# One wide Strassen unit for the values of four retention heads, placed early, in place of two narrow ones

## The chip, the core and the metric

One core of a Trainium2 chip runs the whole program. Its engines work side by side, each through its own list of instructions in order: TensorE (PE) multiplies matrices, VectorE (DVE) and ScalarE (ACT) do elementwise work, GpSimd (POOL) and SyncE (SP) mostly issue transfers. Results of TensorE land in PSUM, which the program uses as 8 banks of 128 partitions by 512 fp32. The metric is the device time of one execution in microseconds, the median of several.

## The reference

A decoder block on 512 tokens of width 1024, cut to what matters here:

```python
h = rmsnorm(x, norm1_w)
proj = h @ w_in                       # 1024 x 6656
rq, rk, rv, rg, mq, mk, mv, ga, gb = split(proj)
rq, rk = rotary(rq), rotary(rk) * RET_DK**-0.5
ret = silu(rg) * retention(rq, rk, rv)        # 4 heads, rv: 256 columns a head, group-normalised
a = ret @ w_ret_out
b = moba_attention(rmsnorm(mq), rmsnorm(mk), mv) @ w_moba_out     # 8 heads of 64
x = x + (sigmoid(ga) * a + sigmoid(gb) * b) @ w_o
h2 = rmsnorm(x, norm2_w)
x = x + (silu(h2 @ w_ffn_gate) * (h2 @ w_ffn_up)) @ w_ffn_down
```

The change concerns `rv`, the 1024 columns of values of the four retention heads.

## The kernel before

Every fp32 operand is kept as a high and a low part, and each product is three matmuls (`mm3`: high x high, high x low, low x high). Most projections run as Strassen units in Winograd's form: seven products B11, T1, T2, B21, B22, T3, T4 of quarter matrices in place of eight. The strings of lines 80 to 84 give their order within a unit; what stands behind the "/" is deferred, and the next unit runs it at its "*1". In the order NORMAL the copy of B11's result seeds the Z bank (`p1`), so that B21 adds onto it there.

A product adds up in a PSUM bank called X, Y, Z (or W), by the table in `wino_unit`. A narrow unit (`cols`, half 256) takes 512 columns of `w_in`; its matmuls are 256 columns wide, and a product needs one bank. A wide unit (half 512) takes 1024 columns; its matmuls are 512 wide, and a product needs two banks. In either there are 168 matmuls (7 products, 8 steps of `mm3`), 12 at a narrow tick and 6 at a wide one: 14 ticks in a narrow unit, 28 in a wide one. Before the change one unit of this part is wide: `mv_ev`, which makes attention's values and half of the retention gates. The bank `zbank` is held for good; of `zbanks` a second one is kept for the first wide unit (`bank`). All other banks come in turn from one pool of eight, for products (`main_ps`, named `pm` in the rows) and for everything else (`side_ps`, named `ps`).

At each tick three things happen: weight pieces move on (`advance`: a ScalarE cast gives the high part `wh`, VectorE's subtraction from it the low part `wl`, and weight sums `raw` + `raw` make T2 and T4), work that was put off comes due (`later`), and one background step is taken from the list `bg` (`run_bg`). The background is attention first: scores of a pair of heads (`att_products`), maxima and exponentials (`att_scores`), transpositions (`att_transpose`, copies `pt` at lines 1130 and 1135), values (`att_values`). Behind it follow the retention scores and values of two heads each (`ret_scores`, `ret_values`), which `rv_out` appends when its unit has given its last result, and `ret_finish` when all four parts in `due` are done.

The order of the units is the list `ORDER` (line 45): a unit of queries and keys, `("rv", 0)`, a gate unit, queries and keys again, `("rv", 1)`, then the others. `weight_plan` puts down the same order for the transfers. A narrow rv unit hands each of its four quarters, two token tiles of one head, to `split`, which makes its high and low parts.

Of the kernel before, what the change touches and what calls it, by code (L numbers as in the profile page):

```python
# [13 lines left out]
ALU = mybir.AluOpType  # L14
# [25 lines left out]
STARTERS = 2  # L40
EXTRA = 1
WIDE = 4
OEXTRA = 5
FEXTRA = -2
ORDER = (("rk", 0), ("rv", 0), ("gb", 0), ("rk", 1), ("rv", 1), ("rg", 1), ("gb", 1), ("b", 0), ("b", 1), ("ga", 0), ("a", 0), ("ga", 1), ("a", 1))
RLAG = (1, 2, 3)
SLAG = (1, 1, 1)
ROT = 1
# [32 lines left out]
ENDING = "B11 T1 *1 T2 B21 B22 T3 T4w"  # L81
PLAIN = "B11 B21 B12 B22"
DOWN = "B11 B21 T1 T2 B22 T3 / T4"
ALONE = "B11 B21 T1 T2 B22 T3 T4z"


def weight_plan():

    units = []

    def feat(blocks):
        assert len(blocks) % 16 == 0  # L100
        for i in range(0, len(blocks), 16):
            units.append(("F", blocks[i:i + 16]))

    def group(name, col, kts):
        return [(name, k * P, col) for k in range(kts)]

    def wino(name1, col1, name2, col2, order=NORMAL):
        quarters = ((name1, col1, 0), (name2, col2, 0), (name2, col2, 4), (name1, col1, 4))
        units.append(("W", [(n, (k0 + k) * P, c + i * P) for n, c, k0 in quarters for i in (0, 1) for k in range(4)],
                      order))  # L110

    halves = (range(4), range(4, 8))

    def cols(col):
        units.append(("X", ("w_in", halves, (col, col + 256), 256), NORMAL))

    units += [("M", (C_MQ, 0)), ("M", (C_MQ, 4)), ("M", (C_MK, 0)), ("M", (C_MK, 4))]
    units.append(("X", ("w_in", halves, (C_MV, C_RG), 512), NORMAL))
    for name, i in ORDER:
        if name == "rg":  # L120
            cols(C_RG + 512 * i)
        elif name == "rv":
            cols(C_RV + 512 * i)
        elif name == "rk":
            wino("w_in", C_RQ + 256 * i, "w_in", C_RK + 256 * i)
        elif name == "a":
            feat(sum([group("w_ret_out", (4 * i + ct) * P, KT) for ct in range(4)], []))
        elif name == "b":
            feat(sum([group("w_moba_out", (4 * i + ct) * P, 4) for ct in range(4)], []))
        else:  # L130
            c = {"ga": C_GA, "gb": C_GB}[name] + 512 * i
            wino("w_in", c + 256, "w_in", c)
    units.append(("X", ("w_o", halves, (0, 512), 512), ALONE))
    for c in range(len(CHUNKS)):
        fs = chunk_tiles(c)
        for f in fs[::2]:
            order = ENDING if f == fs[-2] else NORMAL
            if f < 4:
                order = (PLAIN, DOWN)[f // 2]
            wino("w_ffn_gate", f * P, "w_ffn_up", f * P, order)  # L140
        units.append(("X", ("w_ffn_down", (fs[::2], fs[1::2]), (0, 512), 512), ALONE if c == len(CHUNKS) - 1 else DOWN))
    return units
# [27 lines left out]
def hybrid_block(ctx: ExitStack, tc: tile.TileContext, wall, xin, xtok, n2, cin, out):  # L170
# [642 lines left out]
    def wino_unit(w, ev, hooks={}):  # L813

        u = cur[0]
        cur[0] += 1
        order = plan[u][2].split()
        wide = plan[u][0] == "X" and plan[u][1][3] == 512
        banks = {}

        def bank(b):
            if b not in banks:
                z = zbank if b == "Z" else main_ps()
                banks[b] = [z, zbanks.pop() if b == "Z" and len(zbanks) > 1 else main_ps()] if wide else z
            return banks[b]

        def third(*x):
            ev.c22(*x)
            if "T4w" in order:
                ev.u3(*x)  # L830

        def first(*x):
            ev.p1(*([*x, bank("Z")] if seed else x))

        whole = "T4w" in order or "T4z" in order
        seed = order[1] != "B21"
        table = {"B11": ("X", "A11", True, False, first), "T1": ("Y", "S1", True, False, ev.p5),
                 "T2": ("X", "S2", False, False, ev.u2), "B21": ("Z", "A12", not seed, True, ev.c11),
                 "B22": ("Y", "S4", False, True, ev.c12), "T3": ("X", "S3", False, whole, third),
                 "T4": ("X", "A22", False, True, ev.c21),  # L840
                 "T4w": ("W", "A22", True, True, getattr(ev, "c21w", None)),
                 "T4z": ("Z", "A22", False, True, ev.c21)}

        def run(q):
            b, m, start, stop, out = table[q]
            wino_prod(w, u, bank(b), m, q.rstrip("wz"), start, stop, out,
                      (lambda i: ev.u3(bank("X"), i, bank("Z"))) if q == "T3" and "T4z" in order else None,
                      q == "T4z")

        rest = False  # L850
        for q in order:
            if q == "/":
                rest = True
            elif q[0] == "*":
                for _ in range(int(q[1:])):
                    wino_finish()
            elif rest:
                wpend.append(lambda q=q: run(q))
            else:
                run(q)  # L860
                if q in hooks:
                    hooks[q]()
# [53 lines left out]
    class WideQuarters:  # L916


        def __init__(self, out):
            self.out = out  # L920
            self.tiles = big(nm("qa")), big(nm("qb"))
            self.a, self.b = ((t[:, :512], t[:, 512:]) for t in self.tiles)

        def p1(self, x, i, z):
            A.copy(z[i], x[i])

        def p5(self, y, i):
            A.activation(self.a[i], y[i], AF.Copy, scale=-1.0)
# [2 lines left out]
            A.activation(self.b[i], x[i], AF.Copy, scale=-1.0)  # L931

        def c11(self, z, i):
            self.out(0, 0, i, z[i])

        def c12(self, y, i):
            V.tensor_tensor(self.b[i], self.b[i], y[i], ALU.subtract)
# [268 lines left out]
    def rot_out(h0):  # L1206
        def f(r, c, x):

            a, b = halves(nm("rot"))
            hf = RDK // 2  # L1210
            cos, sin = (y[:, r * 256:(r + 1) * 256].unsqueeze(1).to_broadcast([P, 2, 256]) for y in (cosT, sinT))
            part = {}

            def turn():
                A.copy(b[:hf], x[hf:])
                A.copy(b[hf:], x[:hf])

            def same():
                V.tensor_tensor(two(a), two(x), cos, ALU.mult)

            def high():
                if (c, h0) not in rT:
                    H, L = big(f"rH{c}_{h0}", F32R), big(f"rL{c}_{h0}", F32R)
                    rT[c, h0] = H, L
                    for i in (0, 1):
                        s = slice(i * 512, (i + 1) * 512)
                        (rqT, rkT)[c][h0 + i] = Two(H[:, s], L[:, s])
                part["H"], part["L"] = (two(y)[:, :, r * 256:(r + 1) * 256] for y in rT[c, h0])
                A.copy(part["H"], two(a))

            d = lane_start(LANE)
            if c == 0 or d == 0:
                turn()
            else:
                later(d, turn)
            later(1 if c == 0 else d + 1, same)
            later(d + 1, lambda: V.tensor_tensor(two(b), two(b), sin, ALU.mult))
            later(d + 2, lambda: V.tensor_tensor(a, a, b, ALU.add))
            later(d + 3, high)
            later(d + 4, lambda: V.tensor_tensor(part["L"], two(a), part["H"].bitcast(F32), ALU.subtract))  # L1240
        return f

    rqT, rkT = {}, {}
# [1 line left out]

    rv = {}

    def rv_out(h0):
        def f(pair, i, x):
            rv[h0 + i, pair] = split(f"rv{h0 + i}_{pair}", x, None, 0 if i == 0 else SLAG[1])  # L1250
            if (pair, i) == (1, 0):
                a, b = ([lambda h=h, j=j: ret_scores(h, j) for j in range(NT)] for h in (h0, h0 + 1))
                v, w = ([lambda h=h, p=p: ret_values(h, p) for p in range(2)] for h in (h0, h0 + 1))
                fs = gates(h0 // 2)
                bg.extend(a + fs[:3] + v + b + [fs[3], None, None] + w + [None])
                ret_done("rv")
        return f


    sk = small("sk", RH * NT, 1)  # L1260
# [44 lines left out]
    def ret_values(h, pair):  # L1305
        ps = side_ps()
        for i in (2 * pair, 2 * pair + 1):
            c = (i % 2) * 256
            for j in range(i + 1):
                key, off = sc_off[j]  # L1310
                o = off + (i - j) * P
                mm3(ps[:, c:c + 256], tuple(x[:, o:o + P] for x in sc[h, key]),
                    rv[h, j // 2][:, (j % 2) * 256:(j % 2) * 256 + 256], j == 0, j == i)
        def stats():
            for i in (0, 1):
                bs = tp.tile([P, 6], F32, name=nm("bs"), tag="bs", bufs=4)
# [55 lines left out]

    def rk_unit(n):
        wino_unit(hW, Quarters(rot_out(2 * n)))

    def rv_unit(n):
        wino_unit(hW, Quarters(rv_out(2 * n)))


    sga, sgb, mixT = {}, {}, {}  # L1380
# [74 lines left out]
    def branch(cts, n, mov, evac):  # L1455
# [2 lines left out]
        feat_blocks(blocks[:n] + [wino_finish] + blocks[n:])  # L1458

    make = {  # L1460
        "rg": rg_unit, "rk": rk_unit, "rv": rv_unit,
        "ga": lambda n: gate_unit(sga, 4 * n),
        "gb": lambda n: gate_unit(sgb, 4 * n),
        "a": lambda n: branch(range(4 * n, 4 * n + 4), KT, retT, a_evac),
# [4 lines left out]
    wino_unit(hW, mv_ev)  # L1469
    more_raws(-WIDE)  # L1470
    for name, n in ORDER:
        make[name](n)
    assert not bg


# [362 lines left out]
```

## Time and profile before

| | |
|---|---|
| time, median of 3 runs | 779.18 us (779.07 to 779.64) |
| the profiled execution | 779.37 us, its span 777.6 us |
| granted TensorE clock, mean | 0.999 |
| TensorE, VectorE, ScalarE, GpSimd busy | 99%, 81%, 58%, 9% |
| chain that ended last: TensorE, VectorE, ScalarE | 91%, 4%, 3% |
| moved by transfers | 134.85 MB, 173 GB/s on average |

The span is that of the instructions on the slowest (here the only) core; the execution has 1.77 us around it. Matmuls overlap one another, so the duration of one row is longer than the spacing from one to the next; the spacing is what a matmul costs in a full stream. A row of the timeline can stand for several like instructions (x2, x4), and rows of two kinds overlap where they alternate. In the names `wh` and `wl` are the parts of a weight piece, `hS` and `hA` those of activation sums and quarters, `mk` and `mq` attention's keys and queries, `p` softmax rows, `mx` and `nb` row maxima and what is made of them, `rot` and `rH` rotated queries and keys, `moT` attention's output.

### The profile page before, as it was taken

How to read it: one execution, taken by the hardware profiler on the slowest of the kernel's cores; microseconds unless marked ns; L12 is line 12 of the kernel's file. 1: busy time of each engine (PE TensorE's matmuls, PEld its weight loads, DVE VectorE, ACT ScalarE, POOL GpSimd, SP SyncE). 2: the span in 40 equal slices, each digit the busy share in tenths (PEclk: the TensorE clock that was granted, in tenths of full speed). 3: DMA queues.
4: the chain of work that ended last, by engine and by line, in shares of the span. 5: the costliest groups of instructions: out<-in, count | busy, mean ns of one | idle time of the engine just before them, and what ended most of it. 6: DMA issues, size and time to landing. Idle time of an engine off the chain costs nothing.

```text
span 777.6 us, 13317 instructions
## 1 busy us (share of the span) xinstructions
PE 770.1 (99%) x5226; PEld 702.2 (90%) x5226; DVE 630.9 (81%) x959; ACT 454.7 (58%) x744; POOL 68.7 (9%) x83
## 2 busy tenths in 40 slices
PE   8999999999999999999999999999999999999997
PEld 6888888889999998989988899989999899988996
DVE  6988688987797687758589998899787977789786
ACT  7656587877675485634355775655554455654551
POOL 0001000000101000000001000111001110110000
PEclk9999999999999999999999999999999999999999
DMA  9947542536778475553899714789556993779502
GB/s 324 356 122 186 136 83 56 145 101 163 190 164 203 110 220 117 166 134 119 258 329 248 183 34 116 185 205 304 150 145 156 268 265 99 173 201 294 119 2 109
DMA packets 40671, 134.85 MB, mean 173 GB/s; under 512 B 4512, under 2 KB 5024, under 8 KB 40608
## 3 DMA queue, kind: packets, MB, share of 16 engines
q1 hardware_dynamic: 28512, 93.75, 34.4%
q0 software_dynamic: 11376, 39.06, 28.6%
q10 hardware_dynamic: 720, 1.18, 0.5%
q8 instruction: 41, 0.67, 0.3%
q14 instruction: 22, 0.18, 0.1%
HBM read 131.88 MB, written 2.10 MB: 172 GB/s over the span
## 4 chain that ended last, share of the span: by engine, by line
PE 91%; DVE 4%; ACT 3%; issue 1%; DMA 1%; ACTq 0%
PE pm L222 84%; PE ps L222 8%; DVE h L222 1%; DMA raw<-wall 1%; DVE ws L222 1%; DVE wl L222 1%; ACT wh L418 1%; ACT f L1577 0%; DVE mx L222 0%; ACT p L1098 0%; DVE rot L222 0%; ACT h L1565 0%; DVE gsl L222 0%; ACT L1684 0%; ACT L1098 0%
## 5 line engine op out<-in xcount | busy, mean ns | idle before, releaser
L222 DVE TENSOR_TENSOR wl<-raw,wh 128x1024 fp32r<-128x1024 f32 x209 | 252.5, 1220 | 46.3 <-ACT wh L418 39.4
L418 ACT CAST wh<-raw 128x1024 fp32r<-128x1024 f32 (+1 forms) x230 | 225.6, 1008 | 59.9 <-DVE raw L222 32.4
L222 PE MATMUL pm<-h,wh 128*128 128x256 f32 x1248 | 225.2, 283 | 0.2 <-ACT fa L1650 0.2
L222 PEld LDWEIGHTS pm<-h,wh 128*128 128x128 f32 x1248 | 195.1, 192 | 0.9 <-ACT fa L1650 0.4
L222 PE MATMUL pm<-h,wl 128*128 128x256 f32 x624 | 176.6, 283 | 0.0
L222 PEld LDWEIGHTS pm<-h,wl 128*128 128x128 f32 x624 | 119.7, 192 | 0.0
L345 POOL DMA_DIRECT2D raw<-wall x60 | 53.9, 898 | 453.2 <-DMA raw<-wall 202.9
L222 PE MATMUL pm<-hS,wh 128*128 128x256 f32 x384 | 71.6, 286 | 0.0
L222 PE MATMUL pm<-wh,hA 128*128 128x256 f32 (+1 forms) x256 | 66.8, 337 | 0.0
L222 PEld LDWEIGHTS pm<-hS,wh 128*128 128x128 f32 x384 | 59.9, 191 | 0.3 <-issue 0.2
L222 PE MATMUL pm<-wh,hS 128*128 128x256 f32 (+1 forms) x256 | 57.2, 311 | 0.0
L222 PE MATMUL pm<-hS,wl 128*128 128x256 f32 x192 | 54.3, 283 | 0.0
L222 PE MATMUL pm<-hA,wh 128*128 128x256 f32 x288 | 53.6, 285 | 0.0
L222 DVE TENSOR_TENSOR raw<-raw,raw 128x1024 f32<-128x1024 f32 (+1 forms) x41 | 48.2, 1181 | 0.4
L222 PEld LDWEIGHTS pm<-wh,hA 128*128 128x128 f32 x256 | 44.4, 190 | 4.1
L222 PEld LDWEIGHTS pm<-hA,wh 128*128 128x128 f32 x288 | 45.2, 191 | 0.9 <-issue 0.3
L222 PEld LDWEIGHTS pm<-wh,hS 128*128 128x128 f32 x256 | 42.8, 190 | 2.8 <-issue 0.2
L222 PE MATMUL pm<-wl,hA 128*128 128x256 f32 (+1 forms) x128 | 42.2, 330 | 0.0
L222 PE MATMUL pm<-hA,wl 128*128 128x256 f32 x144 | 40.7, 283 | 0.0
L222 PE MATMUL pm<-wh,gsh 128*128 128x512 f32 x112 | 39.8, 390 | 0.0
L222 PE MATMUL pm<-wl,hS 128*128 128x256 f32 (+1 forms) x128 | 39.6, 309 | 0.0
L222 PE MATMUL pm<-ret,wh 128*128 128x512 f32 x128 | 39.5, 390 | 0.0
(255 smaller groups left out, 1379.6 us busy)
## 6 DMA issues: line engine op xcount, KB each, us to landing
raw<-wall SPq DMA_DIRECT2D x155, 512.0 KB, 5.4
raw<-wall POOLq DMA_DIRECT2D x70, 512.0 KB, 7.2
raw<-wall SPq DMA_DIRECT2D x19, 256.0 KB, 4.0
raw<-wall POOLq DMA_DIRECT2D x9, 256.0 KB, 7.4
xr<-xtok SPq DMA_DIRECT2D x4, 512.0 KB, 7.2
x<-xin SPq DMA_DIRECT2D x7, 256.0 KB, 5.3
out<-xr SPq DMA_DIRECT2D x7, 256.0 KB, 2.1
raw<-wall ACTq DMA_DIRECT2D x4, 256.0 KB, 6.3
```

What stands on the lines that cost most here:

```text
L222: return f(out, *args, **kw)
L345: nc.gpsimd.dma_start(t[:, s], wall[c, :, s], accum_op=ALU.add)
L418: A.copy(h, src)
```

## The change

One unit `rvv` stands in the place of `("rv", 0)` and makes all 1024 columns of `rv`; `("rv", 1)` goes. The unit is wide, with an order of its own, EARLIER, whose B21 is not added onto a seed: `p1` copies B11's two banks into an SBUF tile `qc` (ScalarE), and `c11` adds the Z banks to it (VectorE). During the unit two more weight buffers are in use (`WIDE2`). Its results are split by pair of heads and token tile, heads 2 and 3 forty ticks later (`VLAG`). The background steps of heads 0 and 1 are appended at the unit's end, those of heads 2 and 3 from the last rotation of the second queries-and-keys unit (`ret_heads`).

```diff
-ORDER = (("rk", 0), ("rv", 0), ("gb", 0), ("rk", 1), ("rv", 1), ("rg", 1), ("gb", 1), ...
+ORDER = (("rk", 0), ("rvv", 0), ("gb", 0), ("rk", 1), ("rg", 1), ("gb", 1), ...
+EARLIER = "B11 *1 B21 T1 T2 B22 T3 / T4"
...
+        elif name == "rvv":
+            units.append(("X", ("w_in", halves, (C_RV, C_RV + 512), 512), EARLIER))
...
-        seed = order[1] != "B21"
+        seed = [q for q in order if q[0] not in "*/"][1] != "B21"
...
-        def p1(self, x, i, z):
-            A.copy(z[i], x[i])
+        def p1(self, x, i, z=None):
+            if z:
+                A.copy(z[i], x[i])
+                return
+            if i == 0:
+                self.first[0], self.first[1] = halves(nm("qc"))
+            A.copy(self.first[i], x[i])
...
         def c11(self, z, i):
-            self.out(0, 0, i, z[i])
+            if not self.first:
+                self.out(0, 0, i, z[i])
+                return
+            f = self.first.pop(i)
+            V.tensor_tensor(f, f, z[i], ALU.add)
+            later(1, lambda: self.out(0, 0, i, f))
...
+            if (r, c, h0) == (1, 0, 2):
+                later(d + 5, lambda: ret_heads(2))
...
+    def rv_unit():
+
+        def out(r, c, i, x):
+            t = 2 * r + i
+            later(VLAG if c else 0, lambda: keep(c, t, x))
+            if (r, c, i) == (1, 0, 1):
                 ret_done("rv")
-        return f
+                ret_heads(0)
+
+        def keep(c, t, x):
+            y = split(f"rv{c}_{t}", x, None, SLAG[1])
+            for h in (0, 1):
+                rv[2 * c + h, t] = y, h * 256
+
+        wino_unit(hW, WideQuarters(out))
...
+        if name == "rvv":
+            more_raws(WIDE2)
         make[name](n)
+        if name == "rvv":
+            more_raws(-WIDE2)
```

Three places of the order of instructions show what moved. The first is TensorE's list at the transposition of one head's `p` in the last group of attention, with the unit's products around it; before the change:

```order
L222 MATMUL pm_198_1507<-wh_208_1624,hS41_498 128x256
L222 MATMUL pm_198_1507<-wl_215_1660,hS41_498 128x256
L222 MATMUL pm_198_1507<-wh_208_1624,hS41_498 128x256 x2
L222 MATMUL pm_198_1507<-wl_215_1660,hS41_498 128x256
L222 MATMUL pm_198_1507<-wh_208_1624,hS41_498 128x256
L222 MATMUL ps_236_1853<-cst_79,p_222_1716 128x128 x4
L222 MATMUL pm_188_1420<-wh_219_1698,hS30_526 128x256
```

and after it:

```order
L227 MATMUL pm_236_1759<-wl_221_1639,hS10_415 128x512
L227 MATMUL pm_236_1759<-wh_213_1608,hS10_415 128x512
L227 MATMUL ps_240_1798<-cst_79,p_227_1687 128x128 x4
L227 MATMUL pm_235_1758<-wh_224_1669,hS11_419 128x512
L227 MATMUL pm_235_1758<-wl_228_1697,hS11_419 128x512
L227 MATMUL pm_235_1758<-wh_224_1669,hS11_419 128x512 x2
L227 MATMUL pm_235_1758<-wl_228_1697,hS11_419 128x512
L227 MATMUL pm_235_1758<-wh_224_1669,hS11_419 128x512
L227 MATMUL ps_242_1820<-cst_79,p_230_1711 128x128 x4
L227 MATMUL ps_243_1827<-mk3_832,mq3_562 128x384
L227 MATMUL ps_244_1828<-mk3_832,mq3_562 128x384
```

The transpositions stand beside matmuls of 512 columns now, six at a tick; the first bank they take (`ps_240`) is the one that held `pm_219`, the second Z bank.

The second place is VectorE's list from the row maxima of the group before (`mx` of `ps_221` and of `ps_226`); before the change:

```order
L222 TENSOR_REDUCE mx_1743<-ps_221_1701 128x1
L222 SCALAR_TENSOR_TENSOR nb_1744<-mx_1743,qs_236 128x1
L222 TENSOR_TENSOR rot_214_1657<-rot_214_1657,cs_121 128x512
L222 RECIPROCAL rl_1713<-l_1712 128x1
L222 TENSOR_SCALAR p_222_1716<-p_222_1716,rl_1713 128x512
L222 TENSOR_REDUCE mx_1792<-ps_229_1774 128x1
L222 TENSOR_REDUCE mx_1792<-ps_230_1775 128x1
L222 SCALAR_TENSOR_TENSOR nb_1793<-mx_1792,qs_236 128x2
L222 TENSOR_TENSOR rot_214_1657<-rot_214_1657 128x512
L222 RECIPROCAL rl_1746<-l_1745 128x1
L222 TENSOR_SCALAR p_226_1749<-p_226_1749,rl_1746 128x512
L222 TENSOR_TENSOR wl_232_1819<-raw_179_1360,wh_227_1766 128x1024
```

and after it:

```order
L227 TENSOR_TENSOR rot_220_1636<-rot_220_1636,cs_121 128x512
L227 RECIPROCAL rl_1684<-l_1683 128x1
L227 TENSOR_SCALAR p_227_1687<-p_227_1687,rl_1684 128x512
L227 TENSOR_TENSOR qc_204_1535<-qc_204_1535,pm_17_233 128x512
L227 TENSOR_TENSOR raw_162_1227<-raw_162_1227,raw_180_1362 128x1024
L227 TENSOR_REDUCE mx_1748<-ps_232_1730 128x1
L227 TENSOR_REDUCE mx_1748<-ps_233_1731 128x1
L227 SCALAR_TENSOR_TENSOR nb_1749<-mx_1748,qs_236 128x2
L227 TENSOR_TENSOR rot_220_1636<-rot_220_1636 128x512
L227 RECIPROCAL rl_1708<-l_1707 128x1
L227 TENSOR_SCALAR p_230_1711<-p_230_1711,rl_1708 128x512
L227 TENSOR_TENSOR qc_204_1535<-qc_204_1535,pm_219_1626 128x512
```

Two additions into `qc` and a weight sum `raw` stand in the list; the second addition reads `pm_219`.

The third place is ScalarE's list up to the copies `pt` out of the bank of those transpositions, `ps_236` before the change:

```order
L1098 ACTIVATE p_234_1831,l_1826<-ps_229_1774,nb_1825,qs_236 128x256
L1098 ACTIVATE p_234_1831,l_1826<-ps_230_1775,nb_1825,qs_236 128x256
L1229 CAST rH0_0_1392<-rot_214_1657 128x2x256
L418 CAST wh_235_1851<-raw_203_1582 128x1024
L1130 COPY pt_210_1629<-ps_236_1853 128x2x128
L1135 COPY pt_212_1631<-ps_236_1853 128x256
```

and `ps_240` after it:

```order
L1113 ACTIVATE p_238_1779,l_1774<-ps_232_1730,nb_1773,qs_236 128x256
L1113 ACTIVATE p_238_1779,l_1774<-ps_233_1731,nb_1773,qs_236 128x256
L494 CAST rv0_0_1782<-qc_204_1535 128x512
L1244 CAST rH0_0_1394<-rot_220_1636 128x2x256
L1145 COPY pt_215_1613<-ps_240_1798 128x2x128
L1150 COPY pt_217_1615<-ps_240_1798 128x256
```

A cast of values has come in, and the weight cast stands elsewhere.

## Rows read from the trace of the kernel before

**Rows 1.** The page: busy time of the engines, and the granted clock in 40 slices.

```profile
PE 770.1 (99%) x5226; PEld 702.2 (90%) x5226; DVE 630.9 (81%) x959; ACT 454.7 (58%) x744; POOL 68.7 (9%) x83
PEclk9999999999999999999999999999999999999999
```

**Rows 2.** Waits of TensorE: engine, tile, releaser; us in total, times, longest us.

```profile
PE ps L542 <- DVE warm L222: 1.2, 1, 1.2
...
PE ps L222 <- ACT p L1098: 0.4, 1, 0.4
PE ps L222 <- ACT pt L1135: 0.3, 1, 0.3
...
PE pm L222 <- DVE ml L222: 0.2, 1, 0.2
```

**Rows 3.** TensorE's timeline, two waits: start us, us, instruction, [idle before <- releaser].

```profile
98.09 0.79 PE L222 MATMUL ps<-mk,mq 64*128 64x384 f32 x5 [0.41 <-ACT p L1098]
...
139.44 0.66 PE L222 MATMUL ps<-cst,p 128*128 128x128 f32 x4 [0.29 <-ACT pt L1135]
```

**Rows 4.** TensorE's timeline, matmuls of 256 columns.

```profile
216.08 0.40 PE L222 MATMUL pm<-hS,wh 128*128 128x256 f32 x2
...
216.44 0.40 PE L222 MATMUL pm<-hS,wh 128*128 128x256 f32 x2
```

**Rows 5.** TensorE's timeline, matmuls of 512 columns (the unit `mv_ev`).

```profile
81.05 0.62 PE L222 MATMUL pm<-wh,hS 128*128 128x512 f32 x2
...
81.73 0.62 PE L222 MATMUL pm<-wh,hS 128*128 128x512 f32 x2
```

**Rows 6.** TensorE's timeline: a group's last scores, and the transposition after them.

```profile
144.03 0.96 PE L222 MATMUL ps<-mk,mq 64*128 64x512 f32 x6
...
152.78 0.60 PE L222 MATMUL ps<-cst,p 128*128 128x128 f32 x4
```

**Rows 7.** VectorE's timeline from 145.1 to 154.1 us.

```profile
145.19 0.69 DVE L222 TENSOR_REDUCE mx<-ps 128x1 f32<-128x512 f32 x1 [1.23 <-PE ps L222]
...
146.60 0.68 DVE L222 TENSOR_TENSOR rL<-rot,rH 128x512 fp32r<-128x512 f32 x1
147.19 1.22 DVE L222 TENSOR_TENSOR wl<-raw,wh 128x1024 fp32r<-128x1024 f32 x1
148.33 0.68 DVE L222 TENSOR_REDUCE mx<-ps 128x1 f32<-128x512 f32 x1
...
152.11 1.22 DVE L222 TENSOR_TENSOR wl<-raw,wh 128x1024 fp32r<-128x1024 f32 x1
153.25 0.75 DVE L222 TENSOR_REDUCE mx<-ps 128x1 f32<-128x256 f32 x2
154.03 0.16 DVE L222 SCALAR_TENSOR_TENSOR nb<-mx,qs 128x2 f32<-128x2 f32 x1
```

**Rows 8.** ScalarE's timeline from 154.2 to 157.3 us.

```profile
154.23 0.56 ACT L1098 ACTIVATE p<-ps,nb,qs 128x256 f32<-128x256 f32 x1 [1.37 <-DVE nb L222]
...
155.33 0.61 ACT L1229 CAST rH<-rot 128x512 fp32r<-128x512 f32 x1
155.84 1.05 ACT L418 CAST wh<-raw 128x1024 fp32r<-128x1024 f32 x1
156.78 0.37 ACT L1130 COPY pt<-ps 128x256 f32<-128x256 f32 x1
157.05 0.38 ACT L1135 COPY pt<-ps 128x256 f32<-128x256 f32 x1
```

**Rows 9.** ScalarE's timeline from 127.7 to 129.3 us.

```profile
127.79 1.05 ACT L418 CAST wh<-raw 128x1024 fp32r<-128x1024 f32 x1
128.75 0.36 ACT L1130 COPY pt<-ps 128x256 f32<-128x256 f32 x1
129.01 0.27 ACT L1135 COPY pt<-ps 128x128 f32<-128x128 f32 x1
```

More of the change, by code (lines that the diff above doesn't have):

```diff
@@ L42 @@
 WIDE = 4
+WIDE2 = 2
+VLAG = 40
 OEXTRA = 5
 FEXTRA = -2
-ORDER = (("rk", 0), ("rv", 0), ("gb", 0), ("rk", 1), ("rv", 1), ("rg", 1), ("gb", 1), ("b", 0), ("b", 1), ("ga", 0), ("a", 0), ("ga", 1), ("a", 1))
+ORDER = (("rk", 0), ("rvv", 0), ("gb", 0), ("rk", 1), ("rg", 1), ("gb", 1), ("b", 0), ("b", 1), ("ga", 0), ("a", 0), ("ga", 1), ("a", 1))
 RLAG = (1, 2, 3)
@@ L919, in __init__ @@
         def __init__(self, out):
-            self.out = out
+            self.out, self.first = out, {}
             self.tiles = big(nm("qa")), big(nm("qb"))
             self.a, self.b = ((t[:, :512], t[:, 512:]) for t in self.tiles)
-        def p1(self, x, i, z):
-            A.copy(z[i], x[i])
+        def p1(self, x, i, z=None):
[5 more added lines that the diff above has]
+            A.copy(self.first[i], x[i])
         def p5(self, y, i):
@@ L1246, in hybrid_block, with ret_heads @@
     rv = {}
[L1248 to L1255, printed above, removed]
-                ret_done("rv")
-        return f
+    def rv_unit():
[3 more added lines that the diff above has]
+            if (r, c, i) == (1, 0, 1):
+                ret_done("rv")
+                ret_heads(0)
[4 more added lines that the diff above has]
+        wino_unit(hW, WideQuarters(out))
+    def ret_heads(h0):
+        a, b = ([lambda h=h, j=j: ret_scores(h, j) for j in range(NT)] for h in (h0, h0 + 1))
+        v, w = ([lambda h=h, p=p: ret_values(h, p) for p in range(2)] for h in (h0, h0 + 1))
+        fs = gates(h0 // 2)
+        if h0:
+            bg.extend(a + fs[:2] + v + b + fs[:2] + w)
+            ret_done("rv")
+        else:
+            bg.extend(a + fs[:3] + v + b + [fs[3], None, None] + w + [None])
     sk = small("sk", RH * NT, 1)
@@ L1312, in ret_values @@
                 mm3(ps[:, c:c + 256], tuple(x[:, o:o + P] for x in sc[h, key]),
-                    rv[h, j // 2][:, (j % 2) * 256:(j % 2) * 256 + 256], j == 0, j == i)
+                    rv[h, j][0][:, rv[h, j][1]:rv[h, j][1] + 256], j == 0, j == i)
         def stats():
@@ L1374, in rk_unit @@
         wino_unit(hW, Quarters(rot_out(2 * n)))
-    def rv_unit(n):
-        wino_unit(hW, Quarters(rv_out(2 * n)))
     sga, sgb, mixT = {}, {}, {}
@@ L1460, in hybrid_block @@
     make = {
-        "rg": rg_unit, "rk": rk_unit, "rv": rv_unit,
+        "rg": rg_unit, "rk": rk_unit, "rvv": lambda n: rv_unit(),
         "ga": lambda n: gate_unit(sga, 4 * n),
```

## The prediction

> **What bounds the kernel now.** I read the page first: TensorE is busy for 99% of the span, VectorE for 81%, ScalarE for 58% [rows 1]. Busy time alone doesn't say that nothing waits, so next came the waits of TensorE. Its longest are at the start of the program; in the stretch that the change touches there are two kinds, attention's scores behind a softmax piece `p` and a transposition behind the copy `pt`, 0.4 and 0.3 us in total [rows 2]. The timeline shows where they are, 0.41 us at 98.09 and 0.29 us at 139.44 [rows 3]. So before the change TensorE's own work is the time, in this stretch nearly to the last tenth of a microsecond: what shortens its list is a gain in full, and each new wait on it is a loss in full. I then read, in the order of both programs, which instruction frees the PSUM bank that each attention step takes, and gave those instructions times from the timelines of VectorE and ScalarE.
>
> **The change part by part.** *Fewer, wider matmuls.* The order has 5232 rows of TensorE before and 5064 after: 336 matmuls of 256 columns give way to 168 of 512. Three matmuls of 256 columns start 0.36 us apart (216.08 to 216.44: the two of the first row, and one of the low part between the rows) [rows 4], so one costs 0.120 us. Three of 512 columns take 0.68 us (81.05 to 81.73, in the same pattern) [rows 5], 0.2267 us for one. 336 x 0.120 = 40.32 us go, 168 x 0.2267 = 38.08 us come: **-2.24 us**. The granted clock is in its top tenth in all 40 slices [rows 1], at the upper level of 2.4 GHz, so both prices are at one clock.
>
> The Trainium skill (TensorE: Matmul & The Clock Gate, section Back-to-back issue gap) gives N/2.4 + 2.5 ns as the isolated gap of one matmul of N columns. By that the pairs would be 336 x 0.1092 = 36.69 us and 168 x 0.2158 = 36.26 us, a gain of 0.43 us alone, and the sum below would be 1.8 us worse. The rows don't agree: 120.0 and 226.7 ns [rows 4, 5] lie 11 ns over it at either width, so each matmul that goes is worth more; the sum keeps to the rows.
>
> *Scheduling that stays.* A unit has 28 ticks either way, two narrow units of 14 or one wide one, and each tick takes one background step, so attention's steps are spread alike; they only start beside another unit.
>
> *New waits of TensorE.* A product of a wide unit holds two PSUM banks where a narrow one holds one. With two Z, two X and two Y the unit has 6 of the 8, and attention has 2 left where it had 5 beside a narrow unit. In the order before, no instruction of TensorE waits for a chain that hangs on TensorE's own work of less than 2.7 us earlier (at the spacing above); after the change some seven do. I walked each in the times of before.
>
> The largest is the transposition `ps_240` of one head's `p`. It takes the second Z bank, which comes free at VectorE's second addition into `qc`. In the trace TensorE starts a group's last scores at 144.03 and this transposition at 152.78, 8.75 us later [rows 6]. With the wide unit 24 matmuls of 512 columns lie between in place of 48 of 256, 5.76 - 5.44 = 0.32 us less, and one of the small waits below, 0.25, lies there too. The scores come 0.09 earlier in the walk, at 143.94, so TensorE is there at 143.94 + 8.75 - 0.32 + 0.25 = 152.62. VectorE's list hangs on the same scores: from their maximum at 145.19, which ends an idle time of 1.23 us, 16 instructions follow one another until 152.11, 6.92 us [rows 7]. In the walk they start at 145.10. Behind them the change puts three more ahead of the release: an addition into `qc` (128x512, spacing 0.60 us, as 146.60 to 147.19), a weight sum (128x1024, 1.14 us, as the subtraction 147.19 to 148.33) and the second addition, 0.60: 2.34 us [rows 7]. The bank is free at 145.10 + 6.92 + 2.34 = 154.36, **1.7 us** after TensorE got there. Behind the waiting transposition stands all of TensorE's queue: the unit's next products, and through their outputs everything else.
>
> Next stands the score bank `ps_244`, which waits for ScalarE's copy `pt` out of `ps_240`. Behind the addition VectorE's maxima and `nb` take 0.78 us and 0.08 more (153.25 to 154.03, then `nb`) [rows 7]; ScalarE then has two exponentials (154.23 to 155.33, 1.10 us), the new cast of `rv0_0` and the cast of `rH` (0.51 each, 155.33 to 155.84), and two copies `pt` (0.27 each, 156.78 to 157.05) [rows 8]. From 154.4 that makes 155.25, 156.35, 157.4 and some 158.0; TensorE, after its first stall, is there at 156.85: **1.2 us**.
>
> The smaller ones were walked in the same way. An early second score bank waits for a copy `pt`: before the change ScalarE has a weight cast of 0.96 us (127.79 to 128.75) ahead of the two copies, which end by 129.3 [rows 9]; the new order has the cast later, so they end near 128.3, while TensorE is there near 127.9: 0.4, and 0.1 at the next step. The transpositions after that wait 0.2 beyond what they do now [rows 3]. The unit's second Y bank waits 0.25 for an exponential. A bank for the values waits 0.7 for a copy `pt` that stands behind a product copy and a weight cast of 0.96 [rows 9]. And one transposition waits 0.2 for the low part of `moT`. Together 0.5 + 0.2 + 0.25 + 1.7 + 1.2 + 0.7 + 0.2 = **4.75 us**.
>
> Bounds of these waits: no row of before has this layout of banks. From below they are nothing: the bank order that the trace shows now costs 0.7 us in all [rows 3]. From above each of six (the 0.1 and 0.2 taken as none of their own) is as long as the longest, 6 x 1.7 = 10.2 us. I take the walk, 4.75, because every step of it is a row of this stretch; it is also nearer to the lower end.
>
> *Costed at nothing.* Two copies out of PSUM into a tile take the place of the two into Z on ScalarE. The transfers are as many as before; the weights of the new unit arrive some 19 us ahead of their use in the order, and the waits of TensorE that I show name VectorE and ScalarE, none a transfer [rows 2]. Heads 2 and 3 split their values some 40 ticks later, and their last transpositions stand about 12 x 0.120 + 21 x 0.227 = 6.2 us before they are used; a cast and a low part of about 0.6 us each fit in it. If that cover is gone it costs up to 1 us. Beyond the unit the order shows no new short release.
>
> *Sum.* -2.24 + 4.75 = **+2.5 us**. The profiled execution took 779.37 us, a span of 777.6 and 1.77 around it. 779.37 + 2.5 = 781.9. The median of the runs is 779.18, 0.19 below the profiled one, so I say **781.7 us**.
>
> **The rivals.** *The stalls absorb one another.* While TensorE stands for 1.7 us at `ps_240`, VectorE and ScalarE go on and catch up; every later wait shrinks by what they gained. Left are the early 0.5 and the 1.7: 1.7 + 0.5 - 2.24 = 0, so about 779.2. For it: VectorE is busy for 81% and ScalarE for 58% [rows 1], so there is slack to catch up with. Against it: the wait for `ps_244` hangs on the same VectorE list and so moves along with the first stall instead of shrinking.
>
> *The banks come free in time* (the other side). One mechanism: VectorE's second addition into `qc` ends before TensorE reaches `ps_240`. Then the first stall isn't there and the copy `pt` behind it isn't late. It decides at 152.62: VectorE's list would have to be 1.7 us shorter at that place than in the walk, for which a weight subtraction (1.14 us) and an addition (0.60) [rows 7] that come after it instead of before would do. The small waits, each a fraction of one ScalarE instruction, would have to go as well; then -2.24 is left: 777.0 us. For it speaks that one or two instructions of VectorE decide; against it that their order is fixed in the program and was read from it.
>
> *Every bank wait is like the longest.* 6 x 1.7 - 2.24 = +8: 787.
>
> **How the numbers follow.** Forecast, slower by 2.5 us: 0.52, with a range of its own of 780.6 to 783.8 (the 1.2 and 0.7 may fall to nothing, or each wait may be 0.3 longer). Absorbed, about 779.2: 0.25. Banks free in time, 777.0: 0.18. All like the longest, 787: 0.05. The range that should hold the time reaches from the gain alone, 777.0, to the upper end of the forecast, 783.8, and 0.4 further on either side, since the three runs of before lie 0.57 apart: 776.6 to 784.2. About 0.2% (1.56 us) is what a measurement of this kernel can tell from no change. Faster by more has the chance of its case, 0.18; within it lies the absorbed case, 0.25; slower has the forecast and the worst case, 0.57.
>
> **What would show it.** Matmuls of the retention values of 128x512 at 0.227 us each; then a row of the waits of TensorE for a `ps` tile behind VectorE's `qc` addition, about 1.7 us long, and one behind the copy `pt`, about 1.2 us, both inside the new unit. If the first is not there, the walk of VectorE's list is wrong and the forecast falls with it. If the waits are there but the time is unchanged, the stall was given back elsewhere, and the idle time of TensorE behind the unit would be less than before. A wait that names a transfer, or one for the values of heads 2 and 3, would show a cost that I put at nothing.

## The result and the profile after

The changed kernel takes 783.96 us (median of 6 runs, 783.34 to 787.12) against 779.22 us before (6 runs): +4.74 us between the medians, 0.61%; over all these runs the ratio is 1.0064 with a 95% interval of 1.0053 to 1.0075. The profiled execution took 783.71 us with a span of 781.7, against 779.37 and 777.6.

TensorE's waits of the changed kernel, in the columns of [rows 2]:

```profile
PE ps L227 <- ACT pt L1150: 1.4, 2, 0.8
PE ps L227 <- DVE qc L227: 1.4, 1, 1.4
...
PE ps L227 <- ACT pt L1143: 0.8, 1, 0.8
PE ps L227 <- ACT p L1113: 0.4, 1, 0.4
...
PE pm L227 <- ACT p L1113: 0.2, 1, 0.2
...
PE ps L227 <- DVE moT L227: 0.2, 1, 0.2
```

Where before had two waits in attention's stretch, 0.4 and 0.3 us, there are now seven. The one of 0.4 for `p` is the old one, still ahead of the unit; the old 0.3 has grown to 0.60, and five are new. The six in the unit name what the walk named: the `qc` addition once, the copies `pt` three times, an exponential `p`, and `moT`. The places of five of them in TensorE's timeline (columns as in [rows 3]):

```profile
140.57 0.66 PE L227 MATMUL ps<-cst,p 128*128 128x128 f32 x4 [0.60 <-ACT pt L1150]
...
151.25 0.50 PE L227 MATMUL pm<-wh,hS 128*128 128x512 f32 x1 [0.24 <-ACT p L1113]
...
155.67 0.66 PE L227 MATMUL ps<-cst,p 128*128 128x128 f32 x4 [1.38 <-DVE qc L227]
...
159.34 0.79 PE L227 MATMUL ps<-mk,mq 64*128 64x384 f32 x5 [0.82 <-ACT pt L1150]
...
164.59 1.08 PE L227 MATMUL ps<-pt,mv 128*64 128x512 f32 x4 [0.77 <-ACT pt L1143]
```

VectorE's list at the longest one answers to [rows 7]:

```profile
146.29 0.69 DVE L227 TENSOR_REDUCE mx<-ps 128x1 f32<-128x512 f32 x1 [0.84 <-PE ps L227]
...
151.41 0.68 DVE L227 TENSOR_TENSOR qc<-qc,pm 128x512 f32<-128x512 f32 x1
152.01 1.22 DVE L227 TENSOR_TENSOR raw<-raw,raw 128x1024 f32<-128x1024 f32 x1
153.14 0.48 DVE L227 TENSOR_REDUCE mx<-ps 128x1 f32<-128x128 f32 x2
...
154.94 0.68 DVE L227 TENSOR_TENSOR qc<-qc,pm 128x512 f32<-128x512 f32 x1
155.53 0.75 DVE L227 TENSOR_REDUCE mx<-ps 128x1 f32<-128x256 f32 x2
```

From the maximum at 146.29 to the instruction behind the second addition, at 155.53, VectorE has no gap: 9.24 us, where the walk had 6.92 + 2.34 = 9.26. The transposition follows at 155.67.

ScalarE's list to the copy that frees `ps_244` answers to [rows 8]:

```profile
156.51 0.57 ACT L1113 ACTIVATE p<-ps,nb,qs 128x256 f32<-128x256 f32 x1 [0.67 <-DVE nb L227]
...
157.62 0.61 ACT L494 CAST rv<-qc 128x512 fp32r<-128x512 f32 x1
158.12 0.62 ACT L1244 CAST rH<-rot 128x512 fp32r<-128x512 f32 x1
158.64 0.37 ACT L1145 COPY pt<-ps 128x256 f32<-128x256 f32 x1
158.91 0.38 ACT L1150 COPY pt<-ps 128x256 f32<-128x256 f32 x1
```

The wide matmuls, against [rows 5] and the narrow ones of [rows 4]:

```profile
173.03 0.49 PE L227 MATMUL ps<-cst,p 128*128 128x128 f32 x3
173.27 0.48 PE L227 MATMUL pm<-wh,hS 128*128 128x512 f32 x1
173.59 0.40 PE L227 MATMUL pm<-wl,hS 128*128 128x512 f32 x1
173.82 0.62 PE L227 MATMUL pm<-wh,hS 128*128 128x512 f32 x2
...
174.51 0.62 PE L227 MATMUL pm<-wh,hS 128*128 128x512 f32 x2
```

In the stream three take 0.69 us (173.82 to 174.51), where the forecast had 0.68; but the first one behind a transposition holds the next one off for 0.32 us (173.27 to 173.59) in place of 0.23.

And one row that no part of the forecast had, VectorE's first cast, in the kernel before:

```profile
5.67 0.43 DVE L222 CAST mh<-raw 128x512 fp32r<-128x512 f32 x1 [4.53 <-DMA raw<-wall]
```

and after:

```profile
6.29 0.43 DVE L227 CAST mh<-raw 128x512 fp32r<-128x512 f32 x1 [5.14 <-DMA raw<-wall]
```

The first weight transfer lands 0.62 us later, and all that follows is that much later, up to the unit itself: its first matmul starts at 125.12 instead of 124.48.

**Where the time went.** I lined up TensorE's matmuls of both traces start to start, from the unit's first one (124.48 before, 125.12 after) to the first place from which both programs are alike again (332.78 and 337.29). The start brings +0.64. Waits longer than 0.18 us, in the order of the program: 0.20, 0.77 (0.45 before), 0.35, 1.54, 1.09, 0.93 (0.09), 0.34, less what stood there before: +4.69. The matmuls themselves, each from its start to the next one's: the 336 narrow ones that went took 41.72 us, 0.45 of it the old wait, and the 168 wide ones took 43.15, 2.65 of it waits; that is 41.27 against 40.50, -0.77. The unit products that both programs have took 0.81 less (122.72 and 121.91), where fewer of them stand directly behind a short matmul of the background (41 before, 33 after). Together that is -1.58. The remaining 0.75 are small gaps of attention's and retention's own matmuls, 0.2 and 0.1 of it at one of the retention values. 0.64 + 4.69 - 1.58 + 0.75 = 4.50; the two places are 4.51 apart. After that the distance stays, 0.4 comes back behind the last matmul, and 0.23 is added outside the span: 4.34 from profile to profile.

### The profile page after: what moved, and what is told of

The parts are those of the page before. It is cut to its first block, busy times and chain, and to the rows that moved or that the text cites. A ratio compares the mean times of both kernels' runs of the same rounds, so it can differ in the third digit from the quotient of the medians.

```text
span 781.7 us, 13002 instructions
## 1 busy us (share of the span) xinstructions
PE 771.5 (99%) x5058; PEld 692.9 (89%) x5058; DVE 631.5 (81%) x961; ACT 455.5 (58%) x744; POOL 69.0 (9%) x83
## 4 chain that ended last, share of the span: by engine, by line
PE 89%; DVE 5%; ACT 3%; issue 1%; DMA 1%; ACTq 0%
PE pm L227 82%; PE ps L227 7%; DVE h L227 1%; DVE mx L227 1%; DMA raw<-wall 1%; DVE wl L227 1%; ACT wh L423 1%; DVE ws L227 1%; ACT p L1113 1%; ACT f L1611 0%; DVE rot L227 0%; DVE raw L227 0%; DVE moT L227 0%; DVE p L227 0%; ACT h L1599 0%
## 5 line engine op out<-in xcount | busy, mean ns | idle before, releaser
L227 PE MATMUL pm<-wh,hA 128*128 128x512 f32 (+1 forms) x208 | 64.3, 375 | 0.0
L227 PE MATMUL pm<-wh,hS 128*128 128x512 f32 (+1 forms) x192 | 54.7, 360 | 0.2 <-ACT p L1113 0.2
L227 PEld LDWEIGHTS pm<-wh,hA 128*128 128x128 f32 x208 | 37.8, 189 | 6.0 <-issue 0.2
L227 PEld LDWEIGHTS pm<-wh,hS 128*128 128x128 f32 x192 | 34.2, 189 | 5.5 <-ACT p L1113 0.4
L227 PE MATMUL pm<-wl,hA 128*128 128x512 f32 (+1 forms) x104 | 38.1, 366 | 0.0
L227 PEld LDWEIGHTS pm<-hS,wl 128*128 128x128 f32 x192 | 36.8, 191 | 0.0
```

What stands on the lines that cost most here:

```text
L227: return f(out, *args, **kw)
```

## The experiments

The theory (banks): beside a wide unit attention has two PSUM banks, and its own chain from bank to bank is too slow for that. The rivals: VectorE's additional work is the cause; the early place or the late heads are; the wide unit is slow in itself. All comparisons are with the kernel before on the same chip, 779.26 to 779.38 us.

**The changed kernel again**, unaltered.

> The changed kernel once more, unaltered, so that the others have it beside them on one chip. Its profile showed VectorE's first cast 0.62 us later than before the change, behind the first weight transfer. If that is the program's doing, the cast starts near 6.3 us again and the time is 783.3 to 784.6; if it is one transfer's chance, the cast starts near 5.7 us and the span is some 0.6 us shorter, 781.1.

784.88 us (783.98 to 785.70, 4 runs), 0.9 above the first measurement. The first cast came at 6.32 us again, so the late start isn't one transfer's chance.

**The additions into `qc` one tick earlier.**

```diff
-                    later(1, lambda i=i: out(bank, i))
+                    if q == "B21" and plan[u][2] == EARLIER:
+                        out(bank, i)
+                    else:
+                        later(1, lambda i=i: out(bank, i))
```

> The two additions into qc are issued in the tick in which B21's product ends, not one tick later, so that the second Z bank comes free earlier. Bank theory: the wait for the qc addition (1.4 us in the changed kernel's profile) goes, and the wait for the copy pt behind it (0.8 us or more) shrinks: 1.5 to 2.6 us faster than the changed kernel, 781.4 to 782.5. Rival (the loss is in the spacing of the wide matmuls and elsewhere, and a wait taken away is given back at the next): 783.5 to 784.4.

784.86 us: nothing gained. Its waits of TensorE:

```profile
PE ps L227 <- ACT pt L1153: 1.7, 2, 1.1
...
PE ps L227 <- ACT p L1116: 1.3, 2, 0.9
...
PE ps L227 <- ACT pt L1146: 1.0, 1, 1.0
PE pm L227 <- ACT p L1116: 0.9, 1, 0.9
```

The wait for `qc`, 1.4 us, is gone, and the waits for exponentials and copies in the unit have grown by 2.0. So the loss doesn't hang on that one release: with it out of the way, the next ones in the chain of two banks come late. My expectation missed this; the rival's clause that a wait taken away is given back at the next one held. VectorE still runs both additions here, so its additional work is not cleared by this run.

**The place without the width**: both narrow units early.

```diff
-ORDER = (("rk", 0), ("rv", 0), ("gb", 0), ("rk", 1), ("rv", 1), ...
+ORDER = (("rk", 0), ("rv", 0), ("rv", 1), ("gb", 0), ("rk", 1), ...
...
+            if (r, c, h0) == (1, 0, 2):
+                later(d + 5, lambda: ret_heads(2))
...
```

> The kernel before with its two narrow rv units both placed early, one after the other, and heads 2 and 3 left for the second queries-and-keys unit as in the change: the place without the width. Bank theory: attention keeps its banks, so no wait is new and the time is 779.2, give or take 0.6. Rival (the early place or the late heads cost the time, not the width): 781 to 784.

784.59 us (782.72 to 787.68): by the time alone this speaks for the rival, and the expected 779.2 was missed. The waits of the profiled execution, the fastest of the six (782.72 us, span 780.6), show where its part comes from:

```profile
PE ps L222 <- ACT rH L1229: 1.8, 1, 1.8
...
PE ps L222 <- DVE rL L222: 0.8, 1, 0.8
PE pm L222 <- DVE qb L222: 0.5, 1, 0.5
PE ps L222 <- ACT p L1098: 0.4, 1, 0.4
PE ps L222 <- ACT pt L1135: 0.3, 1, 0.3
```

In attention's stretch stand the two waits of before and no more [rows 2, 3]. What costs the time, 2.0, 1.1 and 0.7 us start to start, lies at 259 and 293 us: the scores of head 2 are reached before their rotated parts are ready. The changed kernel has no such wait, so this run clears the early place of attention's waits but says nothing on its own price in the changed kernel. Four of the other executions had a mean granted clock of 0.995 to 0.998; what made them slower still was not traced.

**Banks held idle beside a narrow unit**: three in the kernel before, from T2 to T3 of the first rv unit.

```diff
...
+        taken = []
+
+        def hold():
+            taken.extend(main_ps() for _ in range(3))
+            for t in taken:
+                V.memset(t[:, 0:2], 0.0)
+
+        def free():
+            for t in taken:
+                A.copy(small("hold", 2), t[:, 0:2])
+
+        wino_unit(hW, Quarters(rv_out(0)), {"T2": hold, "T3": free})
```

> The kernel before with its first narrow rv unit, in which three further PSUM banks are held idle from the end of T2 to the end of T3 (a two-column write at the start, a two-column copy at the end), so that attention has two left as beside the wide unit. Bank theory: waits of ps tiles for exponentials and copies pt appear in that stretch, 2 to 5 us in all: 781.2 to 784. Rival (the waits come of VectorE's additional work, the qc additions and weight sums, not of the banks): 779.2 to 779.8.

785.12 us, +5.8: above the expected band. Waits of TensorE:

```profile
PE ps L222 <- ACT p L1098: 1.7, 3, 0.9
PE ps L222 <- ACT pt L1135: 1.3, 2, 1.0
```

A narrow unit, with no `qc` and no wide matmul in it, gets waits of the changed kernel's kind when attention has two banks. So neither VectorE's additional work nor the width is needed for them; that these two add nothing to the changed kernel's waits is not shown. Matmul by matmul against the kernel before, the stretch is 6.54 us longer: 2.89 of it waits, within the expected 2 to 5, 2.94 matmuls at the lower clock (below), 0.71 other gaps; 0.8 comes back outside it. Another execution took 785.04 us at a mean granted clock of 1.000, so the lower clock is not what the loss hangs on; its waits were not traced.

**Two held.** The same with `range(2)`.

> As with three held banks, but with two, so that attention has three banks beside the first narrow unit. Bank theory: the waits of ps tiles are fewer and shorter than with three held (5.8 us slower than before in all): 779.7 to 783. Rival (holding banks costs by the additional writes and copies alone, whatever their number): the same as with three held, 784.4 to 785.2.

784.51 us, hardly less than with three held: the expectation was too low again, and the time lies in the rival's range. The trace speaks against the rival: in the run with three held the writes take 0.06 us each on VectorE, the copies come only at 166.35 us, behind all of the waits, and no wait of TensorE names them:

```profile
146.61 0.06 DVE L222 MEMSET pm<- 128x2 f32 x2
...
166.35 0.37 ACT L1389 COPY hold<-pm 128x2 f32<-128x2 f32 x3
```

With two held the waits are two for `pt` (1.8 us) and two for `p` (1.3), of which 0.7 were there before; attention waits in fewer places, but in one of them for 1.5 us. Matmul by matmul the stretch is 4.99 us longer: 3.15 of waits, 1.52 at the lower clock, 0.32 other gaps. The waits are no shorter in sum than with three held, so how long they are doesn't follow from the number of banks alone. Four banks for attention were not tried.

**Attention left out of both kernels**, a pair. `att_step` only hands value tiles on as attention's output.

> The kernel before without attention's scores, exponentials, transpositions and values (its output is taken from the value tiles instead, which leaves out that part of the computation). It is one half of a pair: what counts is its difference from the next run, the changed kernel with the same part left out. By the forecast's price of the matmuls the wide one is 2.2 us faster of the two; if wide matmuls are dearer in themselves than the rows said, 0.9 or less; if the loss is in the unit and not in attention beside it, the wide one is slower by 3 us or more.

> The changed kernel without attention's scores, exponentials, transpositions and values, the other half of the pair. Bank theory: no attention step asks for a bank, so the waits of the wide unit are gone, and the gain of the wider matmuls stands alone: 2.2 us below its partner if 0.2267 and 0.120 us hold, less the 0.6 us by which the first weights landed later, if that belongs to the program. Rival: the wide unit is slow in itself, 3 us or more above its partner.

746.38 us and 745.28 us: the wide one is 1.1 us faster of the two. Start to start, from the unit to where the programs are alike again, the 336 narrow matmuls took 40.32 us (0.1200 each), and the 168 wide ones 38.33 (0.2282) without a wait of 0.71: -1.99, near the forecast's -2.24. With that wait, and the unit's start 0.16 us later, it is the 1.1 us. None of the unit's waits for `ps` banks is left (the first two rows are from the start of the program):

```profile
PE ps L547 <- DVE warm L227: 1.2, 1, 1.2
PE pm L227 <- DVE mh L227: 0.8, 1, 0.8
PE pm L227 <- DVE wl L227: 0.5, 1, 0.5
```

There is one for a weight's low part, which this program alone has. Both start late here, the first cast at 6.46 and 6.59 us.

**Attention at half pace** in the unit.

```diff
...
+        if pace["slow"] and pace["n"] % 2 == 0:
+            pace["debt"] += 1
+            settle()
+            return
+        if not pace["slow"] and pace["debt"] and pace["n"] % 4 == 0:
+            pace["debt"] -= 1
+            n += 1
...
```

> The changed kernel, in which attention takes a background step in every second tick of the wide unit, and after the unit an additional step in every fourth tick until it has caught up. Attention has two banks as before, but twice the time for each step. Bank theory: the seven waits in the unit go; four short releases are left behind it, where it catches up, at most 2 us together: 779 to 781.5. If the waits go and nothing replaces them, 779.2 - 0.9 + 0.6 = 779 at the spacing that the changed kernel's trace shows. Rival (the wide unit itself, or the weights, cost the time): 783.5 to 785.

781.17 us, 1.9 above before and 2.8 to 3.7 below the changed kernel (783.96 and 784.88). In the unit one wait is left, and behind it TensorE is slow:

```profile
142.68 0.95 PE L227 MATMUL ps<-mk,mq 64*128 64x384 f32 x5 [1.60 <-ACT pt L1160]
...
144.28 0.63 PE L227 MATMUL pm<-wl,hA 128*128 128x512 f32 x1
144.71 1.05 PE L227 MATMUL pm<-wh,hA 128*128 128x512 f32 x2
145.56 0.63 PE L227 MATMUL pm<-wl,hA 128*128 128x512 f32 x1
```

From 144.28 to 144.71 is 0.43 us for a matmul of 512 columns, which is 512 columns at 1.2 GHz, the lower level.

**Attention paced at chosen ticks.**

```diff
+REST = (3, 7, 9, 13, 15, 18, 21, 24, 27, 30)
...
+        if pace["unit"]:
+            pace["n"] += 1
+            if pace["n"] in REST:
+                pace["debt"] += 1
+                settle()
+                return
...
```

> The changed kernel, in which attention skips ten chosen ticks of the wide unit (3, 7, 9, 13, 15, 18, 21, 24, 27, 30) and takes an additional step in every fourth tick behind the unit until it has caught up. Bank theory: the time between an attention step's release and the next one's need grows at the places that wait, so their 4.7 us shrink to 0 to 2; the start, 0.6 us later than before the change, stays: 783.9 - 4.7 + 1 = 780, from 778.0 if no wait is left to 781.2 if it goes as with half pace. Rival (any pace of attention costs as much somewhere else): 783 or more.

779.12 us (11 runs), a ratio to before of 0.9999 (0.9990 to 1.0008). The program has the wide unit in its early place, the `qc` additions, the late heads, the late start (first cast at 6.22 us), and the same matmuls; only the ticks at which attention's steps come are others. Its waits:

```profile
PE pm L228 <- DVE qc L228: 0.4, 1, 0.4
PE ps L228 <- ACT p L1127: 0.4, 1, 0.4
```

The wait for `p` is the old one, ahead of the unit. The run gives back the whole loss, some 4.8 us: the same unit costs nothing when attention asks for its two banks less often. It doesn't by itself tell the banks from the load of the engines, since steps put off also take their work on VectorE and ScalarE away from the unit; for that stand the held banks. It does not beat the kernel before: in the stretch it is 1.14 us faster (207.16 against 208.30), and the late start takes 0.56 of that.

**No lag** for the values of heads 2 and 3 (`VLAG = 0`).

> The changed kernel with the values of heads 2 and 3 split at once, not forty ticks later. Bank theory: casts and subtractions of 128x512 come into VectorE's and ScalarE's lists while attention runs there, so the waits get a little longer: 784.5 to 786. Rival (the lateness of these values costs the time): 780 to 783.

793.53 us, outside both expectations. The waits in the unit are those of the changed kernel to the tenth; new ones follow when head 2's scores begin:

```profile
PE ps L227 <- ACT rH L1244: 3.9, 1, 3.9
PE ps L227 <- DVE sc L227: 1.8, 2, 1.3
```

So the lag of forty ticks is not what costs the changed kernel its time. Matmul by matmul this run is 10.0 us longer than the changed kernel in the stretch: 7.35 of it waits and 2.0 at the lower clock. Without the lag the wait for `rH` of the run with narrow early units comes back, and longer. Why the lag removes it I didn't settle.

**An idle write at the end** of each kernel, for the late start.

```diff
     assert not bg
+    nc.gpsimd.memset(cp.tile([P, 2], F32, name="tail"), 0.0)
```

> The kernel before with one write of 128x2 values by GpSimd at its very end, which nothing waits for. VectorE's first cast started at 5.52 to 5.67 us in three programs and at 6.13 to 6.6 in six, behind the same first transfers. If the start hangs on the program as a whole and not on the change, it may move here too, with the span: 779.2 to 780.2. If only the changed work moves it, it stays near 5.7 and the time at 779.2.

> The changed kernel with the same idle write at its end. If the late start belongs to the change, the first cast stays at 6.2 to 6.4 us and the time at 783.3 to 785; if it hangs on the program as a whole, it may come at 5.5 to 5.7 and the span be 0.6 us shorter.

779.27 and 783.98 us, the first cast at 5.59 and 6.09 us: each kernel kept its time and its early or late start. In all, five programs with narrow units started at 5.52 to 5.67 us, seven with the wide one at 6.09 to 6.32, and the pair without attention, one of each, at 6.46 and 6.59. It goes with the program; what in it decides stays open.

## Why the prediction was right and wrong

- *What bounds the kernel*: right. Each wait on TensorE was a loss in full, and nothing but 0.4 us behind the last matmul came back.
- *The new waits*: right in place and cause for six of the seven; the early one (0.5) is a gap of 0.20 between two scores at 128.73 and 129.04 us that no row of the waits names. In sum 4.75 us forecast and 4.69 measured (0.5, 0.2, 0.25, 1.7, 1.2, 0.7, 0.2 against 0.20, 0.32, 0.35, 1.54, 1.09, 0.85, 0.34). That the sum agrees to 0.06 is partly luck: single terms are off by 0.10 to 0.30 us, three down and four up. The runs add what the walk didn't see: the waits are one chain, and taking out its longest link moved its time to the others. That a shortage of banks is enough for such waits is shown with the held banks; what share VectorE's additional work has in the 4.69 stays open.
- *Fewer, wider matmuls*, -2.24: near for the unit alone (-1.99 without attention), mis-sized beside attention. The exchange itself gave -0.77, the products that both programs have 0.81 more, -1.58 together. I took both prices from stretches without transpositions. Beside attention a wide matmul costs 0.2411 us and a narrow one 0.1228: 18 of the wide ones stand behind a short matmul and take 0.32 us each, 11 of the narrow ones 0.205.
- *Costed at nothing*: this is the step that failed most, and with the matmuls' price above it is what made the sum too low. I argued the transfers away by their number and by the lead of the unit's weights, and looked at no other transfer; the first one of the program landed 0.62 us later, for +0.64. The small gaps of attention's and retention's own matmuls, +0.75, were not priced at all.
- *The sum*: the sign was right, the size was not, +2.5 forecast and +4.74 measured; 783.96 lies in the wide range, and just above the forecast's own (780.6 to 783.8). The matmuls' 0.66, the start's 0.64 and the gaps' 0.75 make 2.05, which is what the sum lacks: 2.51 + 2.05 - 0.06 = 4.50, the difference in the stretch. The lower end of the forecast's own range was added up wrongly: if the 1.2 and the 0.7 fall to nothing, 781.7 becomes 779.8 and not 780.6. Nothing came to hang on it.
- *The rivals*: the stalls did not absorb one another: the wait for `ps_244` followed the first one as argued against that rival. The banks did not come free in time: TensorE was held at `ps_240` for 1.38 us. Beside the longest wait of 1.54 the next was 1.09 and four were under 0.4, so the worst case fell too.
- The formula of the Trainium skill (TensorE: Matmul & The Clock Gate, section Back-to-back issue gap) gives an estimate of 215.8 ns for a wide matmul and 109.2 for a narrow one. The pair without attention shows 228.2 and 120.0, so the rows were the better price.

## What to carry to other kernels

When a change takes a scarce resource (here PSUM banks) from work that runs beside it, walk the neighbour's release chain instruction by instruction in the old trace's times: that gave 4.75 us of waits where 4.69 came, with errors in single terms that cancelled. Price the changed instructions in the company that they will have, and look for one number that nothing should have moved, as the landing of the first transfer. Where the chain as a whole is too slow, moving one release earlier gained nothing here; asking less often, with attention's steps at chosen ticks, gave back all of it.

## What the hardware showed beyond that

TensorE's clock fell to its lower level behind some waits. Granted clock by stretch, with half pace around the wait of 1.60 us (columns: stretch, us, busy time of TensorE, its weight loads, VectorE, ScalarE, GpSimd, granted clock, share of the transfers, GB/s):

```profile
130.00:142.00 12.00, 11.07 (x75) 9.31 (x73) 9.98 (x25) 9.26 (x22) 0.86 (x1) 1.00 0.63 133
142.50:147.00 4.50, 4.32 (x16) 3.25 (x17) 4.01 (x7) 2.90 (x7) 0.00 (x0) 0.62 0.00 0
147.00:160.00 13.00, 13.00 (x69) 9.22 (x68) 11.99 (x20) 8.38 (x16) 1.72 (x2) 1.00 0.35 58
```

and with three banks held:

```profile
140.00:150.00 10.00, 8.92 (x67) 6.68 (x66) 8.56 (x22) 8.26 (x19) 0.00 (x0) 1.00 0.62 160
150.00:157.00 7.00, 5.74 (x32) 5.38 (x33) 3.68 (x10) 3.00 (x10) 0.86 (x1) 0.60 0.50 125
```

It fell likewise with two banks held (0.74 from 157 to 163 us, around a wait of 1.5 us) and without the lag (0.70 from 262 to 270 us, around one of 3.9). In the changed kernel the clock stayed at 1.00 behind its waits of 1.38 and 0.82 us, and in the profiled run with narrow early units also behind one of 1.8 us, so the length of the wait alone doesn't tell. Where it fell it made the wait dearer: with half pace five matmuls of 512 columns took 0.43 us each in place of 0.23, 1.0 us on top of a wait of 1.6.
